# Moving a unit's query, key and value loads from the load queue to ScalarE's queue

## The chip, the cores and the metric

One core of one Trainium2 chip runs the whole program. The metric is the device time of one execution in microseconds, here the median of three runs. A second execution was recorded by the hardware profiler; all rows below come from it. The engines are named as the profile names them: PE (TensorE matmul), PEld (TensorE weight load), DVE (VectorE), ACT (ScalarE), POOL (GpSimd), SP (SyncE, which only issues transfers). A letter q behind an engine (ACTq, SPq) is its sequencer: the part that waits, and that issues transfers.

## The reference, cut to what matters

Two layers work on 1024 prompt rows and 8 x 16 sample rows of width 1024. The first is a gated unit over chunks of 128 rows, the second an mLSTM block with 4 heads of width 512. The change touches the second layer alone, in this part:

```python
def _mlstm_chunk(carry, inp):
    C, n, m = carry
    q, k, v, ig, lf = inp
    ...
    s = jnp.einsum('bhtd,bhsd->bhts', q, k) * w_intra
    num = jnp.einsum('bhts,bhse->bhte', s, v) + w_inter[..., None] * jnp.einsum('bhtd,bhde->bhte', q, C)
    ...
    C_new = decay[..., None, None] * C + jnp.einsum('bhs,bhsd,bhse->bhde', w, k, v)
...
    h = _layernorm(h, hn_g.reshape(H, DH)).reshape(bsz, t_len, E).astype(xm.dtype)
    out = (h + skip * xc) * jax.nn.silu(z)
    return out @ w_out, (C, n, m, new_conv)
```

For each head and chunk one needs the rows of q, k and v, the decay rows (from which `w_intra` and `w_inter` come), and later, for the gate, the rows of `skip * xc` and `silu(z)`.

## The kernel before, in words

The projections of the second layer write q, k, v, skip and z rows to scratch tensors in HBM (`q_d`, `k_d`, `vb_d`, `sk_d`, `z_d`), and the decay rows to `cw_d`. After that come the units. A `Unit(h, n)` is one head h and one block of 128 prompt rows; there are 4 x 8 of them, and one more for each head holds its sample rows (n = 8; the code calls these four riders, since each rides along in the iteration of a prompt unit). One iteration of the last loop does the numerator and the state update of unit i, the scores and splits of unit i+1, the projection of unit i-2, the gate of unit i-1, and one `Stream`: the update of one 512 x 512 sample state, which is loaded (`c0`, two halves of 512 KB), updated on DVE at line 1148, and stored.

`fetch(units[i + 2], IN)` with `IN = ("qT", "kT", "v", "cw")` loads what unit i+2 needs, `fetch(u, LATE)` with `("sk", "zz")` what unit i's gate needs. Both call `load_qkv`. Each of the tiles qT, kT, vv and cw has two buffers, so a load has to wait until the unit two fetches ago has done with its buffer: qT until POOL has split it (tile q, line 90), kT until PE has transposed it, vv until POOL has split it (tile va, line 90). sk and zz have one buffer.

Five engines work through lists that are in order. PE's list is the order of the code. The lists of the others are made when the program is built: a scheduler with a model of the durations puts each instruction on its engine's list, and a transfer stands in the list of the engine that issues it. `S.dma_start` is SP's list, the load queue; `A.dma_start` is ACT's list. An instruction whose semaphore has not come holds up everything behind it in its list. Transfers report their landing through eight semaphores which SP's and ACT's transfers share in turn, so a transfer may also have to wait until an earlier one on its semaphore has landed.

Before the change SP issues qT, kT, vv, sk, zz, all stream transfers and weights; ACT issues cw and the stores of a few results. Lines that the text speaks of: 89 (`split`, ACT's cast into the high half), 90 (`split`, the low half on DVE or POOL), 877/878 (z rows: SiLU and store), 1044, 1050, 1056 (the loads in `load_qkv`: qT, kT, sk, zz; vv; cw), 1101 and 1107 (`keys` of a sample head, and the stores of st_d, from which the streams' rows sk come), 1127 and 1130 (a stream's loads), 1141 (ev, the stream's PSUM copy), 1150 (its store), 1230 and 1232 (`mask`: cw plus a mask on DVE, Exp on ACT, tile dd), 1271 (scaling of qT), 1329 (hn, copy of the numerator), 1399 (x, the projection added to the rows). The profile drops buffer numbers: sk is both a unit's skip rows and a stream's rows.

Of the kernel before, what the change touches and what calls it, by code (L numbers as in the profile page):

```python
# [15 lines left out]
P = 128  # L16
# [54 lines left out]
def trunk_kernel(ctx: ExitStack, tc: tile.TileContext, ins: dict, outs: list):  # L71
    nc = tc.nc
    order = Order(tc)
    V, A, G, T = nc.vector, nc.scalar, nc.gpsimd, nc.tensor
    T = Ordered(order, T)
    S = nc.sync
# [51 lines left out]
    vb_d = [dram.tile([NT * P, DH], F32, name=f"vb_d{h}") for h in range(H)]  # L128
    sk_d = [dram.tile([DH, NT * P], F32, name=f"sk_d{h}") for h in range(H)]
    z_d = [dram.tile([DH, NT * P], F32, name=f"z_d{h}") for h in range(H)]  # L130
    cw_d = dram.tile([H, 2, NT * P], F32, name="cw_d")
# [5 lines left out]
    def after(ins, prev):  # L137

        tc.add_manual_dep(ins.ins, prev.ins.name, mybir.DependencyInfo(mybir.DependencyClass.NoSync, mybir.DependencyReason.DATA),
                          reason="holds a slot")  # L140
# [123 lines left out]
    def columns_pe(rowA):  # L264
# [17 lines left out]
                  in_=ident[:SL, :SL].unsqueeze(1).to_broadcast([SL, SB, SL]))  # L282
# [181 lines left out]
    for f in range(NF):  # L464
# [8 lines left out]
        for b in range(NB):  # L473
            vh = az.tile([P, 3, P], F32, name="vh", bufs=4)
            c, fo = divmod(f, 4)
# [9 lines left out]
        for i in range(7):  # L485
            rows_out_, late = late, []
            for p in range(2):
# [22 lines left out]
                elif i in (4, 5):  # L510
                    z, q = (e5[p], q1) if i == 4 else (U2[p], q0)
                    V.tensor_tensor(out=z, in0=acc, in1=z, op=ALU.add)
                    t = az.tile([P, QT], F32, name="t", bufs=4)
# [507 lines left out]
    dw = ctx.enter_context(tc.tile_pool(name="dw", bufs=1, reuse_waits="tile"))  # L1021
# [15 lines left out]
    def load_qkv(pool, h, n, want, prev=None, bufs=None):  # L1037

        got = {}
        ts = slice(n * P, (n + 1) * P)  # L1040
        for nm, src in (("qT", q_d), ("kT", k_d), ("sk", sk_d), ("zz", z_d)):
            if nm in want:
                t = pool.tile([P, DC, P], F32, name=nm, bufs=bufs)
                l = S.dma_start(out=t, in_=src[h].rearrange("(c p) t -> p c t", p=P)[:, :, ts])
                if prev is not None:
                    after(l, prev)
                got[nm] = t
        if "v" in want:
            t = pool.tile([P, DH], F32, name="vv")
            l = S.dma_start(out=t, in_=vb_d[h][ts, :])  # L1050
            if prev is not None:
                after(l, prev)
            got["v"] = t
        if "cw" in want:
            t = pool.tile([P, 2, P], F32, name="cw")
            l = (S if pool is dw else A).dma_start(out=t, in_=cw_d[h, :, ts].partition_broadcast(P))
            if prev is not None:
                after(l, prev)
            got["cw"] = t
        return got  # L1060
# [10 lines left out]
    class Dec:  # L1071


        def __init__(self, h, prev):
            self.h = h
            self.g = load_qkv(dw, h, 8, ("qT",), prev, bufs=2)
            self.g.update(load_qkv(dw, h, 8, ("cw",), prev))
            self.ev = []
            kv = self.kv = rawp.tile([P, 2, DH], F32, name="raw")
            loads = (S.dma_start(out=kv[:, 0].rearrange("p (c t) -> p c t", c=DC), in_=k_d[h].rearrange("(c p) t -> p c t", p=P)[:, :, 8 * P:]),  # L1080
                     S.dma_start(out=kv[:, 1], in_=vb_d[h][8 * P:, :]))
            for l in loads:
                if prev is not None:
                    after(l, prev)
            self.nn = dw.tile([SB, DH], F32, name="nn")
            S.dma_start(out=self.nn, in_=ins["state_mlstm_n"][0, :, h])
# [112 lines left out]
    def fetch(u, want):  # L1199
        if u is None:  # L1200
            return
        u.g.update(load_qkv(ld, u.h, u.n, want, bufs=1 if "sk" in want else None))
# [270 lines left out]
    for h in range((ZDEC + 2) // SB + 1, H):  # L1473
        t = stream_at[h * SB - ZDEC] - 1
# [132 lines left out]
```

## Time and profile before

| what | value |
|---|---|
| median of 3 runs | 1933.91 us (1932.88 to 1936.3) |
| the profiled execution | 1929.5 us, of which the span from the first to the last instruction is 1927.8 us |
| PE busy | 1887.7 us, 98% of the span |
| DVE, ACT, POOL busy | 1216.1, 862.4, 674.9 us |
| granted TensorE clock, mean | 0.996 of full speed |
| transfers | 328.20 MB, mean 170 GB/s |

The units run from about 1390 us to the end. PE hardly rests anywhere: of the 510 us from 1390 to 1900 the profile counts about 9 us as idle. A change can therefore give little there, unless PE is made to wait more. The rest of the table says which engines have room: ACT, which gets new work, is busy for less than half of the span, DVE for 63%.

### The profile page before, as it was taken

The page shows a single profiled execution, that of the slowest core. Times are in us where ns is not written, and L with a number is a line of the kernel's source. Part 1 is how long each engine was busy: PE and PEld are TensorE (multiplying, and loading weights), DVE is VectorE, ACT ScalarE, POOL GpSimd, SP SyncE. Part 2 cuts the span into 40 slices and gives each one's busy share as a digit, 9 for nine tenths or more (in the row PEclk, how much of TensorE's full clock was granted, in tenths as well). Part 3 has the DMA queues.
Part 4 walks back from the last instruction along what each step waited for, and adds up shares of the span by engine and source line. Part 5 has one row for each costly group of instructions (what it writes and reads, how often), then busy time and mean ns, then how long its engine had stood idle before and what let it go on. Part 6 is the DMA issues. An engine that isn't in the chain of part 4 may idle for free.

```text
span 1927.8 us, 32016 instructions
## 1 busy us (share of the span) xinstructions
PE 1887.7 (98%) x11553; PEld 1676.0 (87%) x11553; DVE 1216.1 (63%) x2406; ACT 862.4 (45%) x1760; POOL 674.9 (35%) x725
## 2 busy tenths in 40 slices
PE   7999999999999999999999999999999999999998
PEld 6888999999999778888999989888977887788887
DVE  5832567777776454567666655222388687688786
ACT  5422444444444343446655554222354444444564
POOL 2000234444442000024444421100167457457586
PEclk9999999999999999999999999999999999999999
DMA  6222343333334854435555564787898898876543
GB/s 217 93 93 73 96 109 100 100 98 99 101 97 122 263 152 143 131 92 157 152 160 166 164 186 124 240 256 247 263 320 267 263 287 273 262 239 196 153 130 125
DMA packets 345305, 328.20 MB, mean 170 GB/s; under 512 B 28164, under 2 KB 276436, under 8 KB 345148
## 3 DMA queue, kind: packets, MB, share of 16 engines
q1 hardware_dynamic: 278444, 255.72, 43.4%
q10 hardware_dynamic: 66512, 69.85, 11.7%
q8 instruction: 91, 1.49, 0.3%
q14 instruction: 66, 0.54, 0.1%
q0 software_dynamic: 192, 0.59, 0.1%
HBM read 203.07 MB, written 123.02 MB: 169 GB/s over the span
## 4 chain that ended last, share of the span: by engine, by line
PE 79%; DMA 7%; DVE 5%; POOL 3%; ACT 2%; issue 2%; ACTq 0%; SPq 0%; POOLq 0%; DVEq 0%
PE sm L58 79%; DMA cw<-cw_d 1%; POOL Cl L90 1%; DMA out<-c 1%; DMA z_d<-st 1%; DVE c L1148 1%; POOL va L90 1%; DMA kT<-k_d 1%; DMA vv<-vb_d 1%; DMA c<-in_state_mlstm_C 1%; DVE raw L1380 0%; DVE w L90 0%; DMA st_d<-w 0%; POOL q L90 0%; DVE Cst L1297 0%
## 5 line engine op out<-in xcount | busy, mean ns | idle before, releaser
L58 PE MATMUL sm<-xh,w 128*128 128x384 f32 x1536 | 410.4, 341 | 1.8 <-issue 1.2
L58 PEld LDWEIGHTS sm<-xh,w 128*128 128x128 f32 x1536 | 281.0, 188 | 10.0 <-issue 6.5
L58 PE MATMUL sm<-xl,w 128*128 128x384 f32 x768 | 260.1, 339 | 0.0
L58 PE MATMUL sm<-Xh,w 128*128 128x288 f32 x1024 | 216.9, 299 | 4.3 <-ACT c L499 4.3
L58 PE MATMUL sm<-w,o 128*128 128x512 f32 x864 | 209.7, 398 | 2.1 <-ACT o L89 1.2
L58 PE MATMUL sm<-w,os 128*128 128x512 f32 x864 | 200.3, 393 | 4.5 <-ACT os L89 3.5
L58 PEld LDWEIGHTS sm<-w,os 128*128 128x128 f32 x864 | 162.4, 189 | 40.8 <-ACT os L89 6.0
L58 PEld LDWEIGHTS sm<-w,o 128*128 128x128 f32 x864 | 160.0, 188 | 40.2 <-ACT o L89 1.4
L58 PE MATMUL sm<-w,Xh 128*128 128x512 f32 x576 | 180.5, 394 | 0.9 <-DVE w L90 0.9
L58 PEld LDWEIGHTS sm<-Xh,w 128*128 128x128 f32 x1024 | 168.9, 190 | 4.7 <-ACT c L499 4.5
L58 PE MATMUL sm<-S,w 128*128 128x288 f32 x1152 | 163.8, 297 | 0.0
L90 DVE TENSOR_TENSOR w<-r,w 128x512 fp32r<-128x512 f32 x176 | 137.9, 790 | 35.1 <-ACT w L89 34.4
L58 PEld LDWEIGHTS sm<-S,w 128*128 128x128 f32 x1152 | 155.1, 188 | 0.8
L90 POOL TENSOR_TENSOR Cl<-Cst,Ch 128x514 fp32r<-128x514 f32 x96 | 128.7, 1352 | 73.6 <-ACT Ch L89 50.3
L58 PE MATMUL sm<-Xl,w 128*128 128x288 f32 x512 | 151.9, 297 | 0.0
L58 PEld LDWEIGHTS sm<-xl,w 128*128 128x128 f32 x768 | 144.8, 189 | 0.0
L90 DVE TENSOR_TENSOR w<-raw,w 128x1024 fp32r<-128x1024 f32 x43 | 55.9, 1300 | 130.6 <-ACT w L89 126.6
L89 ACT CAST w<-r 128x512 fp32r<-128x512 f32 x176 | 107.2, 618 | 61.5 <-PE sm L58 29.1
L58 PEld LDWEIGHTS sm<-w,Xh 128*128 128x128 f32 x576 | 108.2, 190 | 24.0 <-DVE w L90 1.8
L58 PE MATMUL sm<-w,Xl 128*128 128x512 f32 x288 | 113.0, 392 | 0.0
L90 DVE TENSOR_TENSOR os<-or,os 128x384 fp32r<-128x384 f32 x96 | 52.8, 555 | 88.0 <-ACT os L89 87.8
L58 PE MATMUL sm<-va,k 128*128 128x258 f32 (+1 forms) x768 | 102.9, 284 | 0.5 <-DVE raw L1380 0.4
(310 smaller groups left out, 3643.5 us busy)
## 6 DMA issues: line engine op xcount, KB each, us to landing
c<-in_state_mlstm_C SPq DMA_DIRECT2D x64, 512.0 KB
out<-c SPq DMA_DIRECT2D x64, 512.0 KB
r<-in_a_w_in SPq DMA_DIRECT2D x96, 256.0 KB
or<-o_d SPq DMA_DIRECT2D x96, 192.0 KB
raw<-in_b_w_in SPq DMA_DIRECT2D x32, 512.0 KB
qT<-q_d SPq DMA_DIRECT2D x40, 256.0 KB
vh<-v_d SPq DMA_DIRECT2D x48, 192.0 KB
vb_d<-st ACTq DMA_DIRECT2D x48, 192.0 KB
```

Of the source, the lines that this page charges most:

```text
L58: ins = fn(*args, **kw)
L89: first = A.copy(out=hi, in_=src)
L90: (lo_eng or V).tensor_tensor(out=lo, in0=src, in1=f32(hi), op=ALU.subtract)
L1148: V.scalar_tensor_tensor(out=c0[:, cc], in0=c0[:, cc], scalar=decB[:, d.h, 8 + b:9 + b], in1=pc, op0=ALU.mult, op1=ALU.add)
```

## The change

The transfers of qT, kT and vv for units and riders go from SP's list to ACT's, where cw already is. sk and zz stay on SP, and so does everything that a sample head (`Dec`, pool `dw`) loads. Nothing is computed differently. In the changed kernel line numbers behind 1040 are one higher.

```diff
         got = {}
         ts = slice(n * P, (n + 1) * P)
+        Q = A if pool is not dw and "cw" in want else S
         for nm, src in (("qT", q_d), ("kT", k_d), ("sk", sk_d), ("zz", z_d)):
             if nm in want:
                 t = pool.tile([P, DC, P], F32, name=nm, bufs=bufs)
-                l = S.dma_start(out=t, in_=src[h].rearrange("(c p) t -> p c t", p=P)[:, :, ts])
+                l = Q.dma_start(out=t, in_=src[h].rearrange("(c p) t -> p c t", p=P)[:, :, ts])
...
         if "v" in want:
             t = pool.tile([P, DH], F32, name="vv")
-            l = S.dma_start(out=t, in_=vb_d[h][ts, :])
+            l = Q.dma_start(out=t, in_=vb_d[h][ts, :])
...
         if "cw" in want:
             t = pool.tile([P, 2, P], F32, name="cw")
-            l = (S if pool is dw else A).dma_start(out=t, in_=cw_d[h, :, ts].partition_broadcast(P))
+            l = Q.dma_start(out=t, in_=cw_d[h, :, ts].partition_broadcast(P))
```

PE's list is the same in both kernels. On ACT's list three rows come in for each unit. The first place is the start of the second layer's units, near 1195 us, while PE still works on the z rows. ACT's list before:

```order
L877 ACTIVATE st<-sm 128x384
L878 DMA z_d_110<-st 128x384
L1056 DMA cw<-cw_d 128x2x128 x2
L1232 ACT_TABLE_LOAD
L1232 ACTIVATE dd<-dd,tok 128x128
L1056 DMA cw<-cw_d 128x2x128
L1232 ACTIVATE dd<-dd,tok 128x128
L89 CAST va_12484<-vv 128x2x256
L89 CAST w<-raw 128x1024
L89 CAST w<-raw 128x512
L877 ACT_TABLE_LOAD
L877 ACTIVATE st<-sm 128x384
```

and in the changed kernel, where the same two first rows and the four loads of the first unit stand ahead of these:

```order
L1045 DMA qT<-q_d_94 128x4x128
L1045 DMA kT<-k_d_98 128x4x128
L1051 DMA vv<-vb_d_102 128x512
L1057 DMA cw<-cw_d 128x2x128
L89 CAST va_12484<-vv 128x2x256
L877 ACTIVATE st<-sm 128x384
L89 CAST w<-raw 128x1024
L89 CAST w<-raw 128x512
L878 DMA z_d_110<-st 128x384
L1233 ACT_TABLE_LOAD
L1233 ACTIVATE dd<-dd,tok 128x128
L1057 DMA cw<-cw_d 128x2x128
```

Directly behind these rows in the changed kernel's list, loads of later values stand among the casts, and ahead of the row that the sample head waits for (raw, line 1102, which was line 1101):

```order
L1051 DMA vv<-vb_d_102 128x512
L89 CAST va_12485<-vv 128x2x256
L1233 ACTIVATE dd<-dd,tok 128x128
L877 ACT_TABLE_LOAD
L877 ACTIVATE st<-sm 128x384
L878 DMA z_d_111<-st 128x384
L89 CAST va_12486<-vv 128x2x256
L1051 DMA vv<-vb_d_102 128x512 x2
L877 ACTIVATE st<-sm 128x384
L878 DMA z_d_111<-st 128x384
L1102 ACTIVATE raw<-sm,tok 128x512
L89 CAST w<-raw 128x512
```

What moved: the two Exp rows (dd) come later, behind the casts, and both unit loads and later value loads stand ahead of work that ACT did without them.

The second place is a unit in the middle, on ACT, at 1468 us of the run before. The numbers behind the names tell the buffers apart; kT_15388 and cw_15392 belong to the same later unit. Before:

```order
L1241 ACTIVATE k2_15138<-sm_15133,tok_12408 128x512
L89 CAST s2_15142<-dd_15029 128x128
L89 CAST q2_15148<-qT_14921 128x512
L1056 DMA cw_15392<-cw_d_114 128x2x128
L1117 DMA out_8<-nn_14464 8x512
L1232 ACTIVATE dd_15496<-dd_15496,tok_12408 128x128
L1056 DMA cw_15615<-cw_d_114 128x2x128
L1329 COPY hn_15048<-sm_15032 128x258
```

and in the changed kernel:

```order
L1242 ACTIVATE k2_15138<-sm_15133,tok_12408 128x512
L1045 DMA kT_15388<-k_d1_99 128x4x128
L89 CAST s2_15142<-dd_15029 128x128
L89 CAST q2_15148<-qT_14921 128x512
L1057 DMA cw_15392<-cw_d_114 128x2x128
L1118 DMA out_8<-nn_14464 8x512
L1051 DMA vv_15759<-vb_d1_103 128x512
L1233 ACTIVATE dd_15496<-dd_15496,tok_12408 128x128
L1057 DMA cw_15615<-cw_d_114 128x2x128
L1045 DMA qT_15386<-q_d1_95 128x4x128
L1330 COPY hn_15048<-sm_15032 128x258
```

Three loads have come in: kT ahead of cw, vv ahead of the Exp, and qT ahead of the copy hn. On SP, at the same place, those three are gone from among the streams' transfers. Before:

```order
L1130 DMA c0_15234<-in_state_mlstm_C 128x2x512
L1044 DMA kT_15388<-k_d1_99 128x4x128
L1130 DMA c0_15236<-in_state_mlstm_C 128x2x512
L1050 DMA vv_15759<-vb_d1_103 128x512
L1086 DMA nn_16210<-in_state_mlstm_n 8x512
L1044 DMA qT_15386<-q_d1_95 128x4x128
L1044 DMA sk_15207<-sk_d0_106 128x4x128
```

and in the changed kernel:

```order
L1131 DMA c0_15234<-in_state_mlstm_C 128x2x512
L1131 DMA c0_15236<-in_state_mlstm_C 128x2x512
L1087 DMA nn_16210<-in_state_mlstm_n 8x512
L1045 DMA sk_15207<-sk_d0_106 128x4x128
L1128 DMA sk48_15232<-st_d2_130 48x1024
```

The rows around them keep their order.

## Rows read from the trace of the kernel before

**Rows 1.** Page, part 1: busy us, share of the span, instructions of each engine.

```profile
PE 1887.7 (98%) x11553; PEld 1676.0 (87%) x11553; DVE 1216.1 (63%) x2406; ACT 862.4 (45%) x1760; POOL 674.9 (35%) x725
```

**Rows 2.** The stretch 1390:1900: us, busy PE, PEld, DVE, ACT, POOL; clock, DMA share, GB/s.

```profile
1390.00:1900.00 510.00, 500.89 (x3340) 418.05 (x3339) 408.28 (x898) 246.21 (x491) 317.63 (x288) 1.00 0.75 235
```

**Rows 3.** Who ended PE's waits, 1390:1900: us in total, times, longest; the two largest.

```profile
PE sm L58 <- DVE x L1399: 3.6, 5, 1.7
PE sm L58 <- POOL q L90: 2.3, 5, 0.6
```

**Rows 4.** Who ended SP's waits, 1390:1900, same columns: three of the moved loads'.

```profile
SPq L1044 <- POOL q L90: 35.4, 15, 6.5
SPq L1044 <- PE sm L58: 30.7, 22, 5.4
...
SPq L1050 <- POOL va L90: 28.1, 15, 3.9
```

**Rows 5.** The tile vv, its loads: issue ns min/median/max, first and last start.

```profile
L1050 SPq DMA_DIRECT2D vv<-vb_d x36: 319/364/1960, 1194.4 to 1841.3; - x36
```

**Rows 6.** The chain that ended last, 1185:1230: start, us, what.

```profile
1203.21 1.20 POOL va L90
...
1204.43 4.71 DMA vv<-vb_d
...
1213.61 0.70 ACT raw L1101
...
1226.47 3.68 PE sm L58 x17
```

**Rows 7.** Timeline of ACT, 1188:1227: start, us, what, idle before.

```profile
1202.22 0.40 ACT L1232 ACTIVATE dd<-dd,tok 128x128 f32<-128x128 f32 x1
...
1204.11 1.57 ACT L89 CAST w<-raw 128x1024 fp32r<-128x1024 f32 x2 [0.98 <-DMA raw<-in_b_w_in]
1205.70 1.28 ACT L877 ACT_TABLE_LOAD   x1
...
1207.90 0.62 ACT L89 CAST va<-vv 128x512 fp32r<-128x512 f32 x1 [0.41 <-ACT st L877]
1208.42 0.49 ACT L877 ACTIVATE st<-sm 128x384 f32<-128x384 f32 x1
```

**Rows 8.** Timeline 1400:1425: an issue of cw, and the cast ahead of it in ACT's list.

```profile
1400.72 0.38 ACTq L1056 DMA_DIRECT2D cw<-cw_d  x1
...
1402.40 0.64 ACT L89 CAST q<-qT 128x512 fp32r<-128x512 f32 x1
```

**Rows 9.** Timeline 1465.5:1479, the second place of the change.

```profile
1469.42 0.45 SPq L1044 DMA_DIRECT2D kT<-k_d  x1
1469.42 0.46 ACTq L1056 DMA_DIRECT2D cw<-cw_d  x1
...
1472.12 1.28 POOL L90 TENSOR_TENSOR q<-qT,q 128x512 fp32r<-128x512 f32 x1
...
1475.57 0.29 DVE L1230 TENSOR_TENSOR dd<-cw,m_pr 128x128 f32<-128x128 f32 x1 [4.33 <-DMA cw<-cw_d]
...
1476.37 0.65 ACT L1329 COPY hn<-sm 128x258 f32<-128x258 f32 x2
...
1476.51 0.49 PE L58 MATMUL sm<-sk 48*128 48x512 f32 x1 [1.25 <-DVE x L1399]
```

**Rows 10.** The whole chain: cw issued by SP behind a qT, and cw issued by ACT.

```profile
1549.28 7.12 DMA cw<-cw_d
...
1609.42 6.04 DMA cw<-cw_d
```

**Rows 11.** The whole chain: a stream's store, its next load, and PE behind them.

```profile
1725.41 6.71 DMA out<-c
1732.19 5.86 DMA c<-in_state_mlstm_C
...
1738.79 51.92 PE sm L58 x327
```

## The prediction

> **What bounds the kernel now.** I read the page's engine table first: PE is busy for 98% of the span, ACT for 45%, DVE for 63% [rows 1]. A kernel like that gains only where PE waits, so the next view is the stretch in which the units run. In the 510 us from 1390 to 1900 PE is busy for 500.89 us, so about 9 us are idle there; DVE is busy for 408 of them, POOL for 318, ACT for 246 [rows 2]. Who ended PE's waits says what the 9 us are: 3.6 us behind DVE's row x (the row added to the residual, which frees a PSUM buffer) and 2.3 us behind POOL's lower half of q [rows 3]. No wait of PE is ended by a load of qT, kT, vv or cw. So these loads are not what PE waits for directly; they can act only through DVE, ACT or POOL.
>
> SP is a different matter. While it worked through its list it stood 35.4 us at a load that waited for POOL's q, 30.7 us at loads that waited for PE and 28.1 us at vv loads that waited for POOL's va [rows 4]: 94 us in which everything behind in SP's list, the streams' stores and loads too, was held up. That is what the change takes away from SP and gives to ACT. The question is whether SP's list was late for anybody, and whether ACT can stand there at no cost.
>
> **The change part by part.** There are 36 fetches (32 units, 4 riders), so 108 transfers go over to ACT. An issue takes 0.364 us in the median [rows 5]: 39 us of issuing in all. Four terms follow, each against the profiled execution of 1929.5 us. That execution lies 4.4 us below the median of the three runs, 1933.91, so I add the sum to the median.
>
> Term 1, the start. Near 1195 us a chain runs through ACT: vv lands, the sample head's row raw follows on ACT at 1213.61, then come its split, the stores of st_d and the load of sk, and PE goes on at 1226.47 after waiting [rows 6]. Whatever delays raw delays PE. In the new list ACT needs the weight cast first, whose load SP now issues behind sk and zz: two issues of 0.364 us [rows 5], so the cast starts at 1204.11 + 0.73 = 1204.84 [rows 7]. From there to the end of the last va cast ACT has 1.57 (two casts) + 2 x 1.28 (table loads) + 2 x 0.40 (dd) + 2 x 0.62 (va) + 0.49 (st) = 6.66 us of work [rows 7]: 1211.50. Then the second vv load waits for POOL's va, 1.20 [rows 6], is issued, 0.36, and a last st, 0.49, stands ahead of raw: 1213.55, against 1213.61 now. So in the good case nothing is lost. In the bad case the third vv load is issued only when the casts and one table load are through, at 1207.7, lands 4.71 us later as it does now [rows 6] at 1212.4, and with the cast of 0.62 and the same 2.05 behind it raw starts at 1215.1: +1.5 us. If zz, which waits for a z store, holds up the weight load on SP further, every us counts in full; I allow 1.1 us: +2.6 us. I take +0.6; the range is 0 to +2.6.
>
> Term 2, cw. Until now cw had ACT's queue nearly to itself, and DVE waits for it: at 1475.57 the mask row dd had made DVE idle for 4.33 us, and behind it in DVE's list stood the row x, for which PE then waited 1.25 us [rows 9]. A later cw is passed on to PE in full there. In the new list kT stands ahead of cw on the same queue. How much this costs no row shows directly. The nearest pair is cw issued by SP behind a qT, 7.12 us from issue to landing, against 6.04 us for one issued by ACT alone [rows 10]: +1.1 us is the upper bound per load, since kT goes out about 1 us earlier than cw in the new list, with k2, and a part of it is over by then. The lower bound is 0, because kT shares the transfer engines with cw today as well: both were issued at 1469.42, on two queues [rows 9]. I take 0.4 us, in three places of this kind (1469 [rows 9], 1609 [rows 10] and one later): +1.2 us, range 0 to +3.3.
>
> Term 3, issuing on ACT. ACT's sequencer runs ahead of ACT: the cw load was issued at 1400.72, while the cast that stands ahead of it in the list ran at 1402.40 [rows 8]. Where ACT has work queued, an issue thus costs nothing, and ACT is busy for 48% of the units' stretch. It costs where ACT had run dry: then what stands behind (hn, ev, the casts) comes 0.36 us later, and it would cost as much as SP's waits do if a buffer were not free yet. At the second place it is free: POOL ended its q at 1472.12 + 1.28 = 1473.40, and hn, the row behind the new qT load, started at 1476.37 [rows 9]. What covers the wait is thus ACT's own position in time, well behind the reader of the buffer. I take +0.5; the range is 0 to the case in which one issue per unit with a qT load behind POOL is exposed, 24 x 0.36 = +8.6 us. The long issues of SP, up to 1.96 us [rows 5], are inside this range.
>
> Term 4, what SP gives back. SP loses 94 us of standing. For a gain, a stream's transfer must have been late for PE. One place shows in the chain: a stream's store of 6.71 us, its next load of 5.86 us directly behind it, and PE goes on at 1738.79 [rows 11]. But the load began as soon as the store had landed; SP was not late. The two transfers run with fewer loads of the same queue behind them, so they may be a little faster; I take -0.5. The bound is PE's whole wait behind x, -3.6 us [rows 3].
>
> Sum: 0.6 + 1.2 + 0.5 - 0.5 = +1.8 us. 1933.91 + 1.8 = **1935.7 us**, a change of +0.1%. A difference under 0.2%, 3.9 us, is about what a measurement of this kernel can't tell from none.
>
> A rule bears on terms 2 and 4. The trace shows a cw load of 7.12 us in SP's crowded queue and of 6.04 us in ACT's [rows 10], a small difference. The Trainium skill, page "DMA: Bandwidth & Descriptors", section "Issuing engines are not separate DMA queues", says that transfers of all issuing engines run on the same 16 DMA engines and interleave, and that issuing from several saves only the sequencer's time. By that rule terms 2 and 4 would both be zero, and the sum +1.1 us; the rows allow both signs, and I go by the rows.
>
> **The rivals.**
>
> Slower: ACT stands where SP stood. The waits of SP at the moved loads are 94 us [rows 4]; ACT's list has qT directly ahead of hn, or of the stream's copy ev, in many units, and vv ahead of the Exp. If qT's wait for POOL's q ends 0.36 us or more after ACT gets there, in the 24 units with a qT scaling, that is +8.6 us, and with terms 1 and 2 as taken +10.4: 1944 us. For it: POOL's q ends PE's waits already [rows 3], so POOL is late in these places; moved transfers also wait for landings of SP's transfers on the shared semaphores. Against it: ACT's sequencer runs ahead [rows 8], and ACT is busy for only 48%. It decides from the point where ten of the 24 are exposed.
>
> Faster: with its own queue, qkv no longer waits in SP's, kT and vv go out when their buffer is free, and POOL's va and DVE's rows come earlier. PE's waits behind x and behind POOL's q would go, 3.6 + 2.3 = 5.9 us: 1928 us. For it: 94 us of standing [rows 4]. Against it: PE, DVE and POOL show hardly any wait for these loads in the rows, and what DVE does wait for, cw [rows 9], gets company in its queue. Also in this direction: the same page, section "Queues, rings and completion order", says that each DMA engine takes turns between the queues that have work; by that rule the units' loads would get turns of their own beside the streams' transfers.
>
> Nothing: the loads were never on the path and ACT has room. Then terms 2 to 4 vanish and 1934.5 us is left.
>
> **How the numbers follow.** No measurable change: 0.50, of which 0.35 for my sum and 0.15 for the last rival. Slower, by ACT's standing or by terms 1 and 2 near their upper ends (2.6 + 3.3 = +5.9): 0.29. Faster, by the freed queue: 0.21. The time predicted is that of the likeliest, 1935.7. The range from 1929 to 1944 reaches from nearly all of the faster case to the price of the slower one; the likeliest one's own range is 1930 to 1938.
>
> **What would show it.** Right: PE's list and its 9 us of idle time in the units nearly unchanged; DVE's wait ahead of dd near 1475 still some 4 to 5 us; ACT's busy time the same; PE's restart near 1226 within 1.5 us of now; SP's waits for POOL's q and va gone, and no like sum in ACT's waits. Wrong: rows of ACT (hn, ev, q) idle behind a transfer's landing or behind POOL with tens of us in total, and more PE idle time behind them; or PE's waits behind x gone, and the restart earlier. The prediction fails if ACT's new waits are on the path of every unit, or if DVE's wait for cw turns out to hang on what SP has in its queue.

## The result, and the profile after

The changed kernel takes 1945.63 us in the median of five runs (1943.57 to 1948.12); the kernel before took 1932.88 us beside it (1928.68 to 1936.3). The ratio is 1.0077 [1.0058, 1.0097], about +15 us. The forecast was 1935.7 us, no measurable change; the measured time lies just above its range. Below, a ratio is turned into us as (ratio - 1) x 1930.

The profiled execution took 1944.92 us. The page, part 1 (busy us, share, instructions) of the changed kernel:

```profile
PE 1893.0 (97%) x11553; PEld 1679.4 (86%) x11553; DVE 1215.5 (63%) x2406; ACT 863.3 (44%) x1760; POOL 678.2 (35%) x725
```

No engine has much more work than before [rows 1]: PE is busy for 5 us more, by its clock (below), POOL for 3. The windows (us, busy PE, PEld, DVE, ACT, POOL, clock, DMA share, GB/s): the stretch that answers to [rows 2], and one place in it:

```profile
1390.00:1915.00 525.00, 507.84 (x3354) 422.91 (x3353) 406.18 (x900) 247.74 (x493) 319.21 (x289) 0.99 0.74 229
...
1448.00:1454.00 6.00, 2.99 (x26) 2.79 (x24) 1.39 (x4) 0.66 (x2) 0.00 (x0) 1.00 0.55 154
1454.00:1460.00 6.00, 6.00 (x36) 5.91 (x37) 5.41 (x17) 5.06 (x10) 4.47 (x4) 0.72 0.83 269
```

PE is idle for 525 - 507.84 = 17.2 us, against 9.1: 8 us more. At 1448 it stands for 3 us, and then works for 6 us at a clock of 0.72. With levels of 1.0 (2.4 GHz) and 0.5 (1.2 GHz), 0.72 means that 3.4 of those 6 us are at the lower one, which costs 1.7 us more. Since PE's list is the same in both kernels, the same matmul can be timed in both traces. Its start in the trace after less its start in the trace before:

| start before, us | lag, us | change since the row above |
|---|---|---|
| 1214 | -2.7 | |
| 1223 | +2.8 | +5.5 |
| 1388 | +1.9 | -0.8 |
| 1402 | +5.5 | +3.6 |
| 1429 | +5.7 | +0.2 |
| 1473 | +9.5 | +3.8 |
| 1542 | +9.4 | -0.1 |
| 1570 | +11.8 | +2.4 |
| 1612 | +11.9 | +0.1 |
| 1625 | +13.4 | +1.5 |
| 1682 | +13.7 | +0.3 |
| 1704 | +16.9 | +3.2 |
| end | +15.1 | -1.8 |

So the time is not lost a little in every unit: it is lost at the start (+2.8, counted from the span's start) and in five steps. A single trace is rough: ahead of 1195, where the engines' lists are the same in both kernels, the lag already wanders between -1.8 and +1.0 us. The waits of the changed kernel, 1390:1915 (us in total, times, longest), first PE's, then SP's and DVE's largest:

```profile
PE sm L58 <- DVE Cst L1298: 3.7, 3, 3.0
PE sm L58 <- ACT ev L1142: 3.1, 2, 1.7
PE sm L58 <- POOL q L90: 2.9, 3, 1.8
PE sm L58 <- DVE x L1400: 2.3, 3, 0.9
PE sm L58 <- ACT q L89: 2.1, 1, 2.1
...
SPq L1045 <- DVE raw L1381: 97.1, 20, 11.3
...
DVE dd L1231 <- DMA cw<-cw_d: 38.9, 16, 5.3
```

The same view of the kernel before, 1390:1900, has for DVE:

```profile
DVE dd L1230 <- DMA cw<-cw_d: 18.5, 9, 4.6
```

SP's waits for POOL and PE [rows 4] are gone; it now runs ahead until it stands at sk, whose buffer DVE's row raw must free. PE's wait behind x has shrunk from 3.6 to 2.3 us, and waits behind Cst, ev and ACT's q have come in. DVE waits for cw twice as long as before. Four of the places, from the timeline of the changed kernel (start, us, what, idle before and its releaser); the lag table has them at 1214, 1429, 1612 and 1682 of before:

```profile
1215.56 0.69 ACT L1102 ACTIVATE raw<-sm,tok 128x512 f32<-128x512 f32 x1 [0.40 <-ACT st L877]
...
1216.30 1.02 PE L58 MATMUL sm<-raw,blk 128*8 128x512 f32 x1 [3.97 <-ACT raw L1102]
...
1435.94 0.37 ACTq L1045 DMA_DIRECT2D kT<-k_d  x1
...
1436.47 1.60 ACTq L1045 DMA_DIRECT2D qT<-q_d  x1
...
1438.13 2.31 ACTq L1045 DMA_DIRECT2D kT<-k_d  x1
...
1440.47 0.89 ACTq L1057 DMA_DIRECT2D cw<-cw_d  x1
...
1452.61 0.29 DVE L1231 TENSOR_TENSOR dd<-cw,m_pr 128x128 f32<-128x128 f32 x1 [5.25 <-DMA cw<-cw_d]
...
1453.42 0.48 DVE L1298 SCALAR_TENSOR_TENSOR Cst<-Cst,decB,sm 128x258 f32<-128x258 f32 x1
...
1453.95 0.63 PE L58 MATMUL sm<-va,k 128*128 128x256 f32 x3 [3.01 <-DVE Cst L1298]
...
1622.02 0.48 ACTq L1057 DMA_DIRECT2D cw<-cw_d  x1
...
1628.15 0.29 DVE L1231 TENSOR_TENSOR dd<-cw,m_pr 128x128 f32<-128x128 f32 x1 [4.26 <-DMA cw<-cw_d]
...
1629.10 0.50 PE L58 MATMUL sm<-sk 48*128 48x512 f32 x1 [0.94 <-DVE x L1400]
...
1690.21 2.59 SPq L144 DMA_DIRECT2D raw<-in_b_w_out  x2
...
1692.44 0.49 ACTq L1057 DMA_DIRECT2D cw<-cw_d  x1
...
1699.59 0.29 DVE L1231 TENSOR_TENSOR dd<-cw,m_pr 128x128 f32<-128x128 f32 x1 [4.47 <-DMA cw<-cw_d]
...
1700.40 0.59 ACT L1142 COPY ev<-sm 128x512 f32<-128x512 f32 x1
...
1701.03 1.06 PE L58 MATMUL sm<-ev,selm 128*32 128x512 f32 x1 [1.71 <-ACT ev L1142]
```

and the timeline of the kernel before at the second, third and fourth of them:

```profile
1431.37 0.37 ACTq L1056 DMA_DIRECT2D cw<-cw_d  x1
...
1441.61 0.28 DVE L1230 TENSOR_TENSOR dd<-cw,m_pr 128x128 f32<-128x128 f32 x1
...
1615.55 0.29 DVE L1230 TENSOR_TENSOR dd<-cw,m_pr 128x128 f32<-128x128 f32 x1 [3.64 <-DMA cw<-cw_d]
...
1678.02 0.37 ACTq L1056 DMA_DIRECT2D cw<-cw_d  x1
...
1678.48 2.76 SPq L1050 DMA_DIRECT2D vv<-vb_d  x2
...
1681.29 0.90 SPq L144 DMA_DIRECT2D raw<-in_b_w_out  x2
...
1683.82 0.29 DVE L1230 TENSOR_TENSOR dd<-cw,m_pr 128x128 f32<-128x128 f32 x1 [2.63 <-POOL q L90]
```

Read them in pairs; the landing times are read from the updates of the loads' semaphores in the traces. **At 1216**: ACT's row raw runs 1.95 us later than before [rows 6]. Two vv issues stand ahead of it on ACT and go out between 1212.47 and 1214.62, and PE stands for 3.97 us. **At 1448**: before, ACT's sequencer issued cw 10.2 us ahead of DVE's row; it took 9.31 us to land, so only 0.9 us were to spare, and DVE didn't wait. Now three issues stand ahead of cw on ACT and hold it for 0.37 + 1.60 + 2.31 = 4.3 us (long issues as SP had them [rows 5], now on ACT). cw goes out 9.1 us later than before, 3.4 us more than PE's lag of 5.7, and it takes 12.04 us to land. DVE waits 5.25 us, its row Cst is late, and PE stands for 3.01 us. The three issues alone don't do it. In the run `loop` (below) the same three hold cw for 3.95 us, but it lands in 8.1 us, and DVE hardly waits:

```profile
1447.99 0.29 DVE L1231 TENSOR_TENSOR dd<-cw,m_pr 128x128 f32<-128x128 f32 x1 [0.99 <-DMA cw<-cw_d]
```

There the lag falls by 1.0 us between 1429 and 1473. Why this cw took 12 us in the changed kernel no run shows. **At 1629**: cw's issue comes 0.7 us later than before by PE's lag (1622.02 - 11.9 against 1609.42 [rows 10]); it lands in 6.04 us as before, DVE's wait is 0.6 us longer, and PE stands for x. **At 1701**: line 144 is not a unit's load at all. It is a pair of weight loads for the projection, 512 KB each, on SP. Before, they stood behind two vv loads that waited for POOL, and went out 3.3 us behind cw. Now the vv loads have left SP, so the weights go out 2.2 us ahead of cw; cw, whose issue is also 0.7 us later by PE's lag, takes 7.06 us instead of 5.71 and DVE's wait ends with it, the Exp and ev on ACT follow, and PE stands for 1.71 us. The place near 1546 (before) is a twin of this one.

**At 1395**, from the chain that ended last (start, us, what):

```profile
1388.29 6.76 DMA z_d<-st
...
1395.12 0.31 ACT q L89
```

ACT's cast q stands behind the last z store, and PE behind the cast, for 2.1 us. Before, the same store landed in 4.70 us (issue to landing) and nothing waited. What is new around it are two x loads (line 1536) of 512 KB, issued 0.3 us ahead of it and 0.1 us behind it by SP, which used to stand at kT there.

### The profile page after: what moved, and what is told of

The parts are those of the page before. It is cut to its first block, busy times and chain, and to the rows that moved or that the text cites. A ratio compares the mean times of both kernels' runs of the same rounds, so it can differ in the third digit from the quotient of the medians.

```text
span 1942.8 us, 31985 instructions
## 1 busy us (share of the span) xinstructions
PE 1893.0 (97%) x11553; PEld 1679.4 (86%) x11553; DVE 1215.5 (63%) x2406; ACT 863.3 (44%) x1760; POOL 678.2 (35%) x725
## 4 chain that ended last, share of the span: by engine, by line
PE 79%; DMA 7%; DVE 6%; ACT 3%; POOL 3%; issue 2%; ACTq 1%; SPq 0%; POOLq 0%; DVEq 0%
PE sm L58 79%; DMA cw<-cw_d 3%; POOL Cl L90 1%; DVE Cst L1298 1%; DMA raw<-in_b_w_in 1%; DVE c L1149 1%; DMA z_d<-st 1%; POOL va L90 0%; DVE raw L1381 0%; DMA vh<-v_d 0%; ACTq L1045 0%; DMA bs<-in_a_b_s 0%; DMA r<-in_a_w_in 0%; DVE dn L1344 0%; ACT Ch L89 0%
## 5 line engine op out<-in xcount | busy, mean ns | idle before, releaser
L58 PEld LDWEIGHTS sm<-xh,w 128*128 128x128 f32 x1536 | 281.4, 189 | 10.9 <-issue 8.6
L90 DVE TENSOR_TENSOR w<-r,w 128x512 fp32r<-128x512 f32 x176 | 138.3, 792 | 38.9 <-ACT w L89 38.1
```

The lines of the kernel that those rows point to most:

```text
L58: ins = fn(*args, **kw)
L90: (lo_eng or V).tensor_tensor(out=lo, in0=src, in1=f32(hi), op=ALU.subtract)
```

## The experiments

Six theories run through the expectations: Start (the loads of the first two units), Decay rows (cw behind kT in ACT's queue), Standing (ACT stands where SP stood), Flood (a freed SP sends weights, x and streams earlier, and cw lands later), Queues (it is where loads are issued) and Lists (it is the order in which the scheduler then puts the computing rows).

**Where it is lost.** `start` moves only the loads of the first two units, `loop` all others:

```diff
-        Q = A if pool is not dw and "cw" in want else S
+        Q = A if pool is not dw and "cw" in want and h == 0 and n < 2 else S
```

> Only the loads of the first two units (in the program's row near 1195 us) go to ScalarE's queue; all later units are as before. The trace of the changed kernel shows PE 4.0 us later behind the row raw near 1215 (a wait and then a stretch of lower granted clock). Theory Start (term 1 was far too small): +3 to +4 us on the time before, about 1936 to 1937, with raw later by 2 us and PE's restart near 1226 later by 3 to 4. Theory Decay rows (cw comes late behind kT in the units) and theory Standing (ACT stands at moved loads in the units): no change, within 1 us of before.

> The complement: the first two units' loads stay on the load queue, all later units' go to ScalarE's queue. Theory Start alone: 4 us of the changed kernel's 12.7 go, +8 to +9, near 1941.5, if what happens in the units is independent of the start; if the units' losses were set up by the shifted start, nearly nothing is left, below +3. Theories Decay rows and Standing: PE's waits near 1395, 1412, 1454, 1557 and 1701 of the changed kernel stay, together about 11 us: +8 to +12.

`start` gave 1.0007 [0.9993, 1.002], `loop` 1.0061 [1.0049, 1.0073]: +1.4 us, which can't be told from nothing, and +11.8 us. Most of the loss is in the loop.

**Is it kT ahead of cw?** `cw_lead` issues cw ahead of its own unit's qT and kT on ACT; `cw_to_sp` is the kernel before with cw moved to SP as well, so that all four loads have one queue, but not ACT's:

```diff
+        lead = prev
+        if "cw" in want:
+            l = Q.dma_start(out=t, in_=cw_d[h, :, ts].partition_broadcast(P))
+            lead = l if Q is A else prev
...
-                    after(l, prev)
+                    after(l, lead)
```

> The changed kernel with cw issued ahead of the qT and kT of its own unit on ScalarE's queue; the same transfers on the same queues. Theory Decay rows: DVE's waits ahead of the mask row dd that stand in front of PE's gaps near 1454, 1557 and 1701 shrink from 5 to 7 us to what they were before, and PE gets most of 4.6 + 2.1 + 2.7 = 9.4 us back: +4 to +6 us over before, near 1938. Theory Standing: the moved loads still stand in ACT's list, so +11 to +13, near 1945. Theory Start says nothing of the units; its 4 us stay in either case.

> The kernel before with cw moved the other way: all loads of a unit, cw too, are issued on the load queue, and ACT issues none of them. Theory Decay rows: cw loses its own place and comes behind qT, kT and the streams' transfers, DVE's waits for cw grow from 18.5 us to 40 us or more, and the time rises by +5 to +12 us although nothing was put on ACT. Theory Standing: ACT has less in its list than before, so no change or slightly faster, -2 to +1. Theory Start: no change near 1226 beyond 1 us.

`cw_lead` is slower than the changed kernel: 1.0125 [1.0112, 1.0138], +24 us; DVE's wait for cw stays at 37.2 us (38.9 in the changed kernel). Some 9 of the 24 us are lost in one step at the start (1195 to 1223 of before, where the changed kernel loses 4.0). So the order within a fetch isn't what makes cw late in general. `cw_to_sp` gave 1.0061 [1.0047, 1.0075] with 35.1 us of DVE waiting for cw: with cw on SP's queue its wait grows as well, and so does the time.

**Is it ACT's standing?** `sp_stands` leaves one partition's row of each load on SP (which then stands as before) and sends 127 by ACT; `act_stands` the other way round. With 16 and 112 partitions they are `sp_stands16` and `act_stands16`; `split_sp` cuts 16/112 with both parts on SP, as a control.

```diff
+        parts = ((slice(0, 1), S), (slice(1, P), A)) if U else ((slice(0, P), S),)
...
+                for r, Q in parts:
+                    l = Q.dma_start(out=t[r], in_=src[h].rearrange("(c p) t -> p c t", p=P)[r, :, ts])
```

> The changed kernel, but partition 0 of every moved tile (1 of 128 rows) is loaded by the load queue again, with the same waits; the other 127 rows stay on ScalarE's queue. So SP stands at every moved load as it did before, and ACT has all that the change gave it. Theory Flood (SP, which no longer stands, sends the streams', weight and x transfers earlier; they share the transfer engines with cw and the z stores, whose landings come 1 to 2 us later): most of the loss comes back, +0 to +4 us over before. Theory Standing (ACT's list is held up by the moved issues): as the changed kernel, +11 to +14. The 108 small transfers cost issues of their own on SP, 0.36 us each, which SP has room for.

> The mirror image: partition 0 of every moved tile is loaded by ScalarE's queue, the other 127 rows by the load queue as before. ACT has all the moved issues and their waits, and SP stands as before; nearly no bytes have moved. Theory Flood: SP sends nothing earlier than before, so -1 to +3 us. Theory Standing: ACT's sequencer is held up as in the changed kernel, and cw behind it, +9 to +13. If only the bytes of kT on ACT's queue hold cw up (theory Decay rows), no change.

The pair measured something else: 1.5544 [1.5519, 1.5569] and 1.5298 [1.5272, 1.5323]. The tile vv of `sp_stands`, its loads (issue ns min/median/max):

```profile
L1054 SPq DMA_DIRECT2D vv<-vb_d x36: 231/362/462, 1196.8 to 2853.3; - x36
L1054 ACTq DMA_DIRECT2D vv<-vb_d x36: 223/498/17590, 1210.6 to 2861.2; - x36
```

An issue of the 127-partition part holds ACT's sequencer for up to 17.6 us. The Trainium skill, page "DMA: Bandwidth & Descriptors", section "Why a DMA increments its semaphore by 16 and not by 1", says that a transfer is spread over the largest number of engines up to 16 that divides its partitions, so 127 partitions get one engine. The runs agree with it in direction: the 127-partition loads of `sp_stands` land in 17 to 28 us in the median, the 128-partition ones of the kernel before in 5.5 to 5.9. No trace here shows the number of engines.

> As sp_stands, but 16 of the 128 partitions are loaded by the load queue and 112 by ScalarE's, since a transfer of 127 partitions took 17 to 24 us where one of 128 takes 5.5. SP stands again at every moved load with the waits of before. Theory Flood: most of the loss comes back, +0 to +5 over before. Theory Standing: as the changed kernel, +11 to +14. If a transfer of 112 partitions is slow too, the time is far above both and says nothing.

> The mirror image with 16 partitions on ScalarE's queue and 112 on the load queue: ACT has all the moved issues and waits, and SP stands as before. Theory Flood: -1 to +4 over before. Theory Standing: +9 to +13. If a transfer of 112 partitions is slow too, the time is far above both and says nothing.

> The kernel before with each of the 108 loads of qT, kT and vv cut into 16 and 112 partitions, both issued by SP: what the cutting alone costs, with nothing moved to ACT. sp_stands16 had +20.3 and act_stands16 +24.2 us. Theory Flood: who issues the small parts matters little, so most of their loss is the cut: +14 to +20 here. Theory Standing: the cut is cheap (108 more issues on SP), +1 to +6, and ACT's part in the issues made up the rest.

`sp_stands16` gave 1.0104 [1.0086, 1.0121], `act_stands16` 1.0116 [1.0093, 1.0139], the control alone 1.0092 [1.0073, 1.0112]. Cutting the 108 loads costs about 18 us by itself; the 2 and 5 us above it are within the intervals. These five runs don't tell Standing from Flood.

**One kind of load at a time.** `only_k`, `only_q` and `only_v` move kT, qT or vv alone; the first:

```diff
-                l = Q.dma_start(out=t, in_=src[h].rearrange("(c p) t -> p c t", p=P)[:, :, ts])
+                l = (Q if nm == "kT" else S).dma_start(out=t, in_=src[h].rearrange("(c p) t -> p c t", p=P)[:, :, ts])
...
-            l = Q.dma_start(out=t, in_=vb_d[h][ts, :])
+            l = S.dma_start(out=t, in_=vb_d[h][ts, :])
```

> Of the three moved loads only vv goes to ScalarE's queue; qT and kT stay. SP's standing at POOL's va (28 us) goes. Theory Flood: the weight loads that stand behind vv in SP's list near 1542 and 1681 us of before go out ahead of cw, cw lands 1 to 1.5 us later there and PE loses 2 to 3 us in each: +3 to +6. Theory Standing: only 36 of 108 issues are on ACT, a third of the loss at most, +0 to +4. Theory Decay rows (kT ahead of cw): no change.

> Of the three only kT goes to ScalarE's queue, where it stands 1 to 5 rows ahead of cw in most units; SP's standing at kT for PE (30.7 us) goes, its standing for POOL stays. Theory Decay rows: all of the loss in the units that comes by way of cw, +5 to +9. Theory Flood: the weight loads still stand behind vv, so the places near 1549 and 1692 lose nothing; the x loads near 1386 go out early: +1 to +4. Theory Standing: a third of the issues, +0 to +4.

> Of the three moved loads only qT goes to ScalarE's queue; kT and vv stay, so SP still stands at kT for PE and at vv for POOL. Theory Flood: neither the x loads near 1388 nor the weight loads near 1545 and 1684 go out earlier; cw lands in 5 to 6 us in the two weight places as before: 0 to +2 us. Theory Standing: qT stands directly ahead of hn or ev on ACT in 24 units, so most of what is left of the loss should be here: +4 to +8.

They gave 1.0048 [1.0029, 1.0067], 1.0032 [1.002, 1.0044] and 1.004 [1.0026, 1.0054]: +9.3, +6.2 and +7.7 us. Each alone costs something, and the three add up to more than the whole change, so they don't act apart. `only_q` shows ACT standing. Its timeline:

```profile
1429.48 0.41 SPq L1045 DMA_DIRECT2D sk<-sk_d  x1
...
1436.75 0.37 ACTq L1057 DMA_DIRECT2D cw<-cw_d  x1
1437.16 0.37 ACT L1330 COPY hn<-sm 128x256 f32<-128x256 f32 x1 [3.16 <-DMA sk<-sk_d]
...
1437.59 0.60 PE L58 MATMUL sm<-qT,kT 128*128 128x128 f32 x3 [2.37 <-ACT hn L1330]
```

ACT's issue of cw had to wait for the landing of SP's sk, 7.2 us after its issue, on the semaphore that both use; hn stands behind that issue, and PE waits 2.37 us for hn. Not all of this run's loss is of that kind: at 1410 PE waits 2.02 us for POOL's q, ahead of which the new order of POOL's list has a row Cl. The changed kernel has that wait too (1.81 us), and so has `before_newlists` below (1.68 us), which moves no transfer.

**Is it the weights?** `early_w` is the kernel before, with SP's weight loads put right behind kT, ahead of vv: the flood without the change. `w_act` is the changed kernel with those loads issued by ACT behind vv, so that they go out late again. `qv_w` is `w_act` with kT left on SP; `late_w` the kernel before with the weights issued by ACT behind cw. The edit of `w_act`:

```diff
-        ld_ = S.dma_start(out=raw.rearrange("p (a b) -> p a b", b=view.shape[2]), in_=view)
+        ld_ = (A if behind else S).dma_start(out=raw.rearrange("p (a b) -> p a b", b=view.shape[2]), in_=view)
+        if behind:
+            after(ld_, behind[0])
```

> The kernel before, all queues as before, but in SP's list the two weight loads of 512 KB (tile raw, four pairs in the units) are put directly behind kT, ahead of vv and qT, in the six places where SP stood at vv for POOL's va first. So they go out about when cw does, not 1.4 to 3.3 us behind it. In the seven runs so far cw lands in 3.4 to 6.0 us where the weights come behind it and in 5.2 to 8.4 where they come ahead or together (first five places). Theory Flood: near 1545 and 1684 us, where DVE waits for cw with no slack, cw lands 1 to 2 us later and PE loses 2 to 3 us with the slower clock behind the wait: +3 to +6 over before. Theories Standing and Decay rows (ACT's list): nothing has changed on ACT, so within 1 us of before.

> The changed kernel, with the same weight loads issued by ACT behind its vv loads, so again behind cw as they were before the change. Theory Flood: cw near 1549 and 1692 lands in 5 to 6 us, not 7; PE gets back 2.4 + 3.2 us there: 4 to 6 us less than the changed kernel, near +8 over before. Theory Standing: ACT has twelve issues more and loses nothing or a little more: +12 to +15.

> The changed kernel with kT left on the load queue and the weight loads issued by ACT behind vv: qT and vv are still moved, both floods are gone (SP stands at kT, the weights go out behind cw). Theory Flood: 0 to +3 over before. Theory Standing: two thirds of the moved issues are on ACT, +5 to +8, hardly less than w_act with +8.

> The kernel before with only the weight loads of the units issued by ACT, behind cw. They go out some 5 us behind cw, not 1.4 to 3.3, and cw should land about 1 us earlier in the two places near 1545 and 1684 (4.3 to 4.7 us where w_act had them so, 5.7 before). Theory Flood: PE's waits there, 0.4 us each and what follows, go: 0 to -2 us, which this measurement may not tell from nothing. If the weights come late for the split that the projection needs, ACT stands at its casts and it is +1 to +4.

`early_w` gave 1.004 [1.0027, 1.0054], +7.7 us, with no load of a unit moved to another queue. `w_act` gave 1.0041 [1.0026, 1.0057], +7.9 us where the changed kernel has +14.9. The difference, 6.9 us, has an uncertainty of 4.8 (half-widths 0.00195 and 0.00155, added in squares). The timeline of `early_w`:

```profile
1680.19 0.93 SPq L146 DMA_DIRECT2D raw<-in_b_w_out  x2
...
1680.57 0.37 ACTq L1063 DMA_DIRECT2D cw<-cw_d  x1
...
1689.04 0.29 DVE L1237 TENSOR_TENSOR dd<-cw,m_pr 128x128 f32<-128x128 f32 x1 [6.46 <-DMA cw<-cw_d]
...
1689.98 0.63 PE L58 MATMUL sm<-ev,selm 128*32 128x512 f32 x3 [2.84 <-DVE x L1406]
```

and of `w_act` at the same place:

```profile
1688.57 0.49 ACTq L1064 DMA_DIRECT2D cw<-cw_d  x1
...
1692.93 1.05 DVE L1238 TENSOR_TENSOR dd<-cw,m_pr 128x128 f32<-128x128 f32 x1 [1.68 <-DMA cw<-cw_d]
...
1694.03 0.82 ACTq L146 DMA_DIRECT2D raw<-in_b_w_out  x2
...
1694.64 0.63 PE L58 MATMUL sm<-ev,selm 128*32 128x512 f32 x3
```

Both places of this kind side by side (near 1545 and 1684 of before). The lead is the issue of the first weight load less that of cw, the landing is from cw's issue, and the step is PE's lag behind the place less the lag ahead of it:

| kernel | weights behind cw, us | cw lands after, us | PE's step, us |
|---|---|---|---|
| before | +3.3, +3.3 | 5.72, 5.71 | 0 |
| only_k | +2.8, +2.8 | 5.07, 4.68 | 0.0, -0.2 |
| only_q | +3.3, +3.3 | 4.53, 6.27 | -0.4, +0.3 |
| w_act | +5.5, +5.5 | 4.72, 4.26 | -0.1, 0.0 |
| changed | -2.3, -2.2 | 6.97, 7.06 | +2.4, +3.2 |
| only_v | -1.6, -2.0 | 7.27, 6.56 | +2.8, +1.7 |
| early_w | -0.2, -0.4 | 8.58, 8.37 | +4.0, +3.8 |

Weights ahead of cw or with it: cw lands in 6.6 to 8.6 us and PE loses 1.7 to 4.0 us. Weights 2.8 us or more behind it: 4.3 to 6.3 us and nothing lost. In `early_w` the two steps, 4.0 + 3.8, are as large as its whole loss by the median; its one trace ends at +4.0, since PE gets some of it back elsewhere. The other kernels with the weights ahead of cw go the same way, but not by the same amount: in `loop`, `cw_lead` and `after_oldlists` (below) cw lands in 6.1 to 8.4 us, and the steps are 0.1 and 2.5, 0.4 and 5.9, 0.9 and 1.6 us. With the weights 2.4 us or more behind it (`start`, `cw_to_sp`, `qv_w`, `late_w`, `before_newlists`) cw lands in 4.1 to 6.0 us, and PE's lag over these waits grows by 0.9 us at most, apart from 2.4 and 2.6 us in `before_newlists` and `late_w`, which arise behind 1556, after the first place. `qv_w` gave 1.0044 [1.0027, 1.0062]; `late_w` 1.0034 [1.0017, 1.005], slower than the kernel before though cw landed in 4.83 and 4.48 us at these places: it loses 2.6 us behind 1556 and 2.6 us near 1739 instead.

**Queues or lists?** The scheduler also puts computing rows in another order when the loads move. `after_oldlists` keeps the changed queues but holds the computing rows of DVE, POOL and ACT in the order of before; `before_newlists` the reverse.

```diff
+    for pins in PINS:
+        held = [f"I-{n}" for n in pins if f"I-{n}" in seen]
+        for p, n in zip(held, held[1:]):
+            tc.add_manual_dep(seen[n], p, ...
```

> The changed kernel, with the computing rows of DVE, POOL and ACT held in the order of the kernel before (all of DVE's and POOL's rows, ACT's rows without its transfers); only where the transfers stand in ACT's and SP's lists is as the scheduler puts them with the change. Theory Queues (Flood and Standing): as the changed kernel, +10 to +14 over before. Theory Lists (the new order of the computing rows costs the time): +0 to +4. If both have a part, between: the weight loads near 1549 and 1692 us, which go out early by SP's list, should cost their 2 to 3 us each in any case, so not under +4 by theory Flood.

> The mirror image: the kernel before, its transfers on their old queues, with the computing rows of DVE, POOL and ACT held in the order of the changed kernel. Theory Queues: 0 to +2. Theory Lists: +8 to +13. Where POOL's state row now stands ahead of q near 1410 us, PE should wait 1.2 us longer by the order alone (the row's 1.29 us), so +1 at least if only such rows count.

`after_oldlists` gave 1.0094 [1.0071, 1.0118], +18 us, `before_newlists` 1.0021 [1.0009, 1.0033], +4.1 us. By its trace `after_oldlists` loses some 9 us at the start, like `cw_lead`, and 11.1 us from 1230 on, where the changed kernel loses 13.2. So with the new queues the old order saves little or nothing, and the new order costs some 4 us without them: most of the loss goes with the queues, a part of it may be the order's.

No version beat the kernel before, and of the eighteen only `start` can't be told from it. Some that move no load of a unit to another queue lose 4 to 8 us too (`before_newlists`, `late_w`, `early_w`). So a part of each of these losses may be what any other order costs this kernel; no run separates that. More was lost than any theory had allowed in `cw_lead`, `only_v`, `early_w`, `late_w`, `after_oldlists` and the four runs with cut loads on two queues.

## Why the prediction was wrong

**What held.** PE's list and the engines' work are as they were. The price is not paid in each unit, as the slower rival had it with its 24 exposed issues: ACT's idle time behind landings is 8.7 us in the units (vv 5.6, z 1.6, st_d 1.5), where it was 9.0, and its waits behind POOL are no longer than before. The loss does go along the way that term 2 described: cw, DVE's dd, then x or Cst or ACT's ev, then PE.

**Term 4 failed, by its sign.** "What SP gives back" was put at -0.5, with bounds of -3.6 and 0: it asked only whether SP's list had been late for anybody. It didn't ask what SP had been keeping back. SP's standing at vv had held two weight loads until 3.3 us behind cw's issue, and its standing at kT the next x load until 3.1 us behind the last z store. Freed, they go out into the same transfer engines ahead of what is urgent. The weights cost 2.4 + 3.2 = 5.6 us in the trace of the changed kernel, and 6.9 +- 4.8 by the timing of `w_act`; that one is shown, since `early_w` makes the loss alone, `w_act` takes it away, and the table above has the step only where the weights go out ahead of cw or with it. The x loads cost up to 3.6 us at 1391; no run moved them alone, but the step there is 2.5 to 4.6 us in the kernels that take kT from SP with the weights left there (the changed one, `loop`, `only_k`, `cw_lead`, `after_oldlists`) and 0.4 to 0.7 us in `qv_w`, `only_v` and `only_q`, which leave kT on SP. (In `w_act`, where SP doesn't stand at kT either but the next x load goes out 0.9 us behind the store, it is 0.2 us. In `late_w`, which moves no unit's load, it is 1.5 us, so the size is not certain.) The prediction's last sentence named this way of failing, "DVE's wait for cw turns out to hang on what SP has in its queue", and gave it no price. The rule of the Trainium skill that it weighed (page "DMA: Bandwidth & Descriptors", section "Issuing engines are not separate DMA queues"), that all queues interleave on the same engines, was right in just this sense: cw on ACT's queue is not sheltered from SP's transfers, 6.6 to 8.6 us against 4.3 to 6.3 in the table. It was read as a reason for zero. The second half of the rule, that a second issuing engine saves only the sequencer's time, doesn't hold here, since that sequencer's standing had set the order of transfers.

**Term 2 was mis-sized, and its cause was seldom the one.** It took +1.2, at most +3.3, for a kT ahead of cw. DVE's wait for cw grew by 20.4 us, and PE lost 3.8 + 2.4 + 1.5 + 3.2 = 10.9 us at the four places behind it. At two of these it is the weights; `cw_lead` doesn't help. At 1629, term 2's own second place, cw goes out 0.7 us later and PE loses 1.5 us where 0.4 were taken; how much depends on how soon cw then lands, since `after_oldlists`, with the same late issue, loses 0.3 us with a landing in 5.1 us, and `before_newlists`, with one 0.6 us late, 2.8 us with 6.7. At 1448 cw is late by its issue (3.4 us) and by its landing (2.7 us), and the cause of the second part is open. At term 2's first place, 1475, PE's wait for x fell from 1.25 to 0.70 us. The bound of +1.1 us per load was too narrow from the start: it came from two loads, while the cw loads on ACT's own queue took 2.9 to 9.3 us in the units of the kernel before.

**Term 3 was too low, as far as can be told.** +0.5 was taken, near the lower end. "ACT's sequencer runs ahead" was right in the rows shown, but a load issued ahead is not yet a load in time: at 1431 10.2 us of lead were 0.9 us to spare. One stand of ACT is shown, 2.37 us for PE in `only_q`, by a wait for a shared semaphore. What the change costs without the weights, `w_act`'s +7.9, `qv_w`'s +8.5 and `only_q`'s +7.7, is as large as the 8.6 of the slower rival, but not by 0.36 us in each unit. How these 8 us divide among ACT's stands, late loads and the order of the lists stays open.

**Term 1 was about right in size**: +0.6 (0 to 2.6) against 1.4 in `start`, within its error. In the changed kernel's one trace its bad case came (raw at 1215.56, where that case had 1215.1), and the restart near 1226 is 1.9 us later, beyond the 1.5 us that were set as a sign. **What the sum left out** is PE's clock behind a wait. Directly behind five waits of the changed kernel (1216, 1395, 1454, 1557 and 1701) the lag grows on, by 1.5, 1.5, 1.7, 1.5 and 1.4 us while PE is busy, at a granted clock of 0.72 in 1454:1460: 7.6 of the 15 us.

The forecast's chance for slower was 0.29. With the weights' 5.6 us in term 4, 1.8 + 0.5 + 5.6 = +7.9 us would have been beyond the bound of 3.9.

## What to carry to other kernels

A queue that stands is also a valve: before its standing is taken away, list what is queued behind it in the next microseconds, how large it is, and which transfer with no slack is then on its way. A sequencer that runs ahead gives its lead to every load that it issues, but what counts is the lead less the time that the load itself takes: each load put in front of an urgent one uses that rest up, by its issue and by its wait for a buffer or for a semaphore that another queue shares. Taking 94 us of standing from SP gained nothing here, and four cw loads that came 0.7 to 6.1 us late cost PE 10.9 us: look first at the paths of DVE and ACT that have no slack to PE.

## What was not expected of the hardware

The clock behind a wait is not set by the length of the wait alone. At the same matmul, behind nearly the same wait, `late_w` and the kernel before differ. Timeline of `late_w`:

```profile
1746.68 0.79 PE L58 MATMUL sm<-sk 48*128 48x512 f32 x1 [1.75 <-DVE x L1406]
```

its windows:

```profile
1745.00:1750.00 5.00, 3.32 (x13) 2.88 (x14) 5.00 (x12) 1.09 (x3) 2.16 (x2) 0.65 0.58 168
1750.00:1755.00 5.00, 5.00 (x31) 5.00 (x31) 3.74 (x10) 0.80 (x2) 1.83 (x2) 0.67 0.86 298
```

and the windows of the kernel before, where PE goes on at 1738.79 [rows 11] after a wait of 1.68 us:

```profile
1737.00:1742.00 5.00, 3.32 (x24) 2.93 (x24) 5.00 (x12) 0.98 (x3) 2.28 (x2) 1.00 0.75 236
1742.00:1747.00 5.00, 5.00 (x40) 4.70 (x39) 5.00 (x13) 1.50 (x3) 2.36 (x3) 1.00 0.84 292
```

PE is busy for 3.32 of 5 us in both; the granted clock is 0.65 and then 0.67 in the one, 1.00 in the other. `late_w` loses 2.6 us there (1731 to 1746 of before) with a wait that is no longer than before. So a wait of 1.7 us costs here either itself alone or itself and more than that again, and no row read here tells which it will be. The other surprise is the 127-partition transfer above: 17.6 us of a sequencer for one issue.
